# Projections that give way every six matmuls instead of every three, and a shift of 224 bytes in the tiles of the last stage

## The chip, the core and the metric

The program runs on one core of a Trainium2 chip. The metric is the device time of one execution in microseconds (us). Three executions of the kernel before took 650.53, 650.55 and 651.75 us; the median, 650.55 us, is the time before.

## What is computed

One decoder block over 1024 tokens and a width of 1024. An RMS norm is followed by one input projection whose columns feed two groups of heads: eight heads of stick-breaking attention (width 64) and four heads of a gated delta rule (width 128, in chunks). Each group's output is normalised per head and multiplied by a gate; one output projection over both groups, a residual and a last RMS norm end the block.

```python
h = rmsnorm(x, norm1_w)
sb_q, sb_k, sb_v, sb_z, g_q, g_k, g_v, g_z, g_b, g_a = split(h @ w_in)
# attention, strictly causal, per head
z = q @ k.T / 8
attn = where(causal, exp(log_sigmoid(z) - tail), 0)   # tail: suffix sums of softplus(z)
o_sb = rmsnorm(attn @ v, sb_norm_w) * silu(sb_z)
# gated delta rule: conv4 + silu on q, k, v, l2 norms, then chunk after chunk
v_new = u - w @ state
o = (q * exp(g)) @ state + a @ v_new
state = state * exp(g_last) + (k * exp(g_last - g)).T @ v_new
o_gdn = rmsnorm(o, gdn_norm_w) * silu(g_z)
out = rmsnorm(x + concat(o_sb, o_gdn) @ w_out, final_norm_w)
```

## The kernel before

All fp32 products that matter are made of three fp32r matmuls: each operand is split into a high and a low part, and `mm3` adds high times high, high times low and low times high. A projection of 128 columns over 1024 tokens is two halves of 512 tokens, each half eight steps over the contraction (k = 0 to 7), each step one `mm3`: 24 matmuls of 128x512 into one PSUM bank `pp`. In their names `xh` and `xl` are the two parts of the activations, `weh` and `wel` those of the weights.

The order of the work is not written by hand. The kernel is made of generators (streams): the projections (`fill`), the delta rule's loads, preparation, solve and scan, the attention windows (`window`), and the output stage. A planner (`Model` and `interleave`) keeps its own clock and its own costs for every engine. Whenever the planner's PE queue is empty it takes, of the streams that are ready, the one of the lowest number, runs it up to its next `yield`, and records the instructions that it issued; this fixes the order of the instructions on each engine. A stream that yields an operation is ready again only when that operation's result has, by the planner's clock, been there for a slack of 450 ns. The projections have number 100, behind attention (about 10) and the delta rule (0 to 0.7), so that they fill PE where nothing else is ready; the products of the output stage have 101 and 102 and take that part later.

The names that the text uses on PE, the engine of the matmuls:

- `pp<-xh,weh`, `pp<-xl,weh`, `pp<-xh,wel`: projections. The list `ORDER` takes the attention's gates, `z0` to `z3`, last of all.
- `pz<-kh,q` and `pz<-kl,q`: scores of an attention window, `kh` and `kl` against a block of queries. ScalarE and VectorE read them (`sgf`, `cc`), GpSimd multiplies, and PE turns the result: `pz<-step,stf`. `ah` and `al` are its two parts; `po<-ah,v2a` and `po<-al,v2a` multiply them with the values; `pz<-step,otf` turns the output back.
- `pc<-state,kqf`, `pc<-xct,xinv`, `pz<-v,kn`, `pz<-state,kqf`, `pz<-vr,at`: one chunk of the delta scan; between the first three a VectorE operation stands each time.
- `pp<-woh,mh`, `pp<-wol,mh`, `pp<-woh,ml`: the output stage. `mh` and `ml` are parts of the activations (the operand that is loaded into the array), `woh` and `wol` those of the output weights (the operand that streams). The delta half (k = 4 to 7 of the 1024 rows of `w_out`) is multiplied first for all eight blocks of tokens, then the attention half (k = 0 to 3).

The weights of the delta half lie in pool `f0`, those of the attention half in pool `f1`, on the other side of the memory, together with `yj`, a scratch tile for squares, and tiles for the residual. In the built program `mh` and `ml` and the delta half's weights all start at a byte address that leaves 128 when divided by 256; the attention half's eight weight tiles leave 96 (`woh0` is at 133728). Of the projections, `xh`, `xl`, `weh` and `wel` all leave 96.

The line of every instruction that the planner records is 358, so the profile's groups are told apart by the names of their tiles.

Of the kernel before, what the change touches and what calls it, by code (L numbers as in the profile page):

```python
# [10 lines left out]
F32 = mybir.dt.float32  # L11
# [6 lines left out]
P = 128  # L18
# [3 lines left out]
NK = D // P  # L22
# [451 lines left out]
def block(tc, xT_d, x_d, n1_d, wE_d, wQ_d, wC_d, conv_d, alog_d, dtb_d, mixw_d, wo_d, fnw_d, out_d):  # L474
# [4 lines left out]
    with ExitStack() as top:  # L479
# [36 lines left out]
        def rsqrt(y, a, n):  # L516
            return G.tensor_tensor(y, a, half[:, 0:n], ALU.pow)
# [68 lines left out]
        def mm3(out, lh, ll, rh, rl, start, stop):  # L586
            TE.matmul(out, lh, rh, start=start, stop=False)
            TE.matmul(out, lh, rl, start=False, stop=False)
            TE.matmul(out, ll, rh, start=False, stop=stop)
# [176 lines left out]
        def values():  # L766
            for b in range(NB):
                yield lambda: ps.room("pp", 2)
                bs = slice(b * P, (b + 1) * P)
                pt = pp()  # L770
                for k in range(NK):
                    mm3(pt[:, 0:256], xh[:, k, bs], xl[:, k, bs], chl[k][:, 0, 264:520], chl[k][:, 1, 264:520], k == 0, k == NK - 1)
                    if k % 2 and k < NK - 1:
                        yield
                v_evac(pt, b, 0, 4, 1.0)
                yield
            flags["v1"] = True
# [107 lines left out]
        def projections():  # L885
            todo = []
            for step in ORDER:
                if step[0] == "G":
                    h = int(step[1])
                    todo += [(f"G{h}{kind}", lambda: True) for kind in (1, 0, 2)]  # L890
                else:
                    todo.append((step, lambda: True))

            def take():
                for n, (name, ok) in enumerate(todo):
                    if ok():
                        del todo[n]
                        if name[0] == "v":
                            return name, None
                        e = {"k": 0, "z": 16}.get(name[0])  # L900
                        e = 4 + 4 * int(name[2]) + int(name[1]) if name[0] == "G" else e + int(name[1])
                        if e == early.e:
                            return name, early
                        cols = Columns(e)
                        cols.load()
                        return name, cols
                return None

            def split(nxt, n):
                while nxt and nxt[1] and len(nxt[1].hl) < n:  # L910
                    nxt[1].split()

            nxt = take()
            split(nxt, 2)
            while nxt:
                name, cols = nxt
                if name[0] == "v":
                    nxt = take()
                    split(nxt, 2)
                    yield from values()  # L920
                    continue
                fill.prio = 100
                for half in range(2):
                    hs = slice(half * 512, (half + 1) * 512)
                    wide = name[:2] == "G0" and half
                    yield lambda: ps.room("pz", 4) if wide else ps.room("pp", 2)
                    pt = pz() if wide else pp()
                    for k in range(NK):
                        n = 8 * half + k
                        if n == 2:  # L930
                            nxt = take()
                        if n == 8:
                            split(nxt, 1)
                        if n == 12:
                            split(nxt, 2)
                        h, l = cols.hl[k // 4]
                        mm3(pt, h[:, k % 4, :], l[:, k % 4, :], xh[:, k, hs], xl[:, k, hs], k == 0, k == NK - 1)
                        if k < NK - 1:
                            yield
                    if half == 0:  # L940
                        if name[0] == "G":
                            ev = g_evac(int(name[1]), int(name[2]))
                        else:
                            ev = {"k": k_evac, "z": z_evac}[name[0]](int(name[1]))
                    flags[name if half else name + ".0"] = ev(pt, half)
                    yield
                if nxt is None:
                    nxt = take()
                    if nxt is None and todo:
                        yield lambda: any(ok() for _, ok in todo)  # L950
                        nxt = take()
                    split(nxt, 2)
            flags["proj"] = True
# [413 lines left out]
        pools = {}  # L1367
# [55 lines left out]
        def block_tile(b, name):  # L1423
            return pools[0].tile([P, D], F32, tag="xr", bufs=3, name=name) if b < 3 else pools[1].tile([P, D], F32, tag="yr", bufs=5, name=name)
# [88 lines left out]
        def products_attention():  # L1513
            yield lambda: f"d{NB - 1}" in flags
            for b in range(NB):
                last = b == NB - 1
                parts = (slice(0, 512), slice(512, 832), slice(832, D)) if last else (slice(0, 512), slice(512, D))
                sy = None
                for got in product(b, 0, parts):
                    if not isinstance(got, tuple):  # L1520
                        yield got
                        continue
                    n, hs, yp, y = got
                    if sy is None:
                        sy = pools[0].tile([P, 3], F32, tag="sy", bufs=2, name="sy")
                        yf = block_tile(0, "yf") if last else y
                    V.tensor_tensor(y[:, hs], yp, y[:, hs], ALU.add)
                    junk = pools[1].tile([P, 512], F32, tag="yj", name="yj")
                    if n == 2:
                        V.scalar_tensor_tensor(junk[:, 0:hs.stop - hs.start], y[:, hs], 1.0 / D, y[:, hs], ALU.mult, ALU.mult, accum_out=sy[:, n:n + 1])  # L1530
                    else:
                        A.activation(junk[:, 0:hs.stop - hs.start], y[:, hs], AF.Square, scale=D ** -0.5, accum_out=sy[:, n:n + 1])
                    if last and n < 2:
                        G.tensor_tensor(yf[:, hs], y[:, hs], wts["fnw"][:, hs], ALU.mult)
                    if n == 1 and last:
                        G.tensor_tensor(sy[:, 0:1], sy[:, 0:1], sy[:, 1:2], ALU.add)
                    elif n:
                        V.scalar_tensor_tensor(sy[:, 0:1], sy[:, 0:1], EPS, sy[:, n:n + 1], ALU.add, ALU.add)
                    if n < len(parts) - 1:
                        yield  # L1540
                        continue
                    if last:
                        V.tensor_tensor(yf[:, hs], y[:, hs], wts["fnw"][:, hs], ALU.mult)
                    ry = pools[0].tile([P, 1], F32, tag="ry", bufs=2, name="ry")
                    os_ = slice(b * P, (b + 1) * P)
                    if last:
                        rsqrt(ry, sy[:, 0:1], 1)
                        V.tensor_scalar(yf[:, 0:640], yf[:, 0:640], ry[:, 0:1], None, ALU.mult)
                        A.activation(yf[:, 640:D], yf[:, 640:D], AF.Copy, scale=ry[:, 0:1])
                        S.dma_start(out_d[os_, 0:640], yf[:, 0:640])  # L1550
                        nc.scalar.dma_start(out_d[os_, 640:D], yf[:, 640:D])
                    else:
                        rsqrt(ry, sy[:, 0:1], 1)
                        for u in range(2):
                            us = slice(512 * u, 512 * u + 512)
                            yb = (pc, po)[u]()
                            A.activation(yb, y[:, us], AF.Copy, scale=ry[:, 0:1])
                            V.tensor_tensor(y[:, us], yb, wts["fnw"][:, us], ALU.mult)
                        S.dma_start(out_d[os_, :], y)
                    ck.free(*ready[b, 0][:2], y)  # L1560
                    flags[f"a{b}"] = True
                    yield

        fill = Stream(projections(), 100, RESULT)
        pre = Stream(delta_pre(), 0.7, DELTA + 0.7)
        interleave(ck, lambda: ps.room("pz", 4),
# [42 lines left out]
```

## Time and profile before

| | us |
|---|---|
| median of three runs | 650.55 |
| the profiled execution | 650.36 |
| its span, first to last instruction | 648.4 |
| outside the span (650.36 - 648.4) | 2.0 |
| PE busy | 639.2 of 648.4 |
| VectorE (DVE) busy | 423.4 |
| ScalarE (ACT) busy | 393.7 |
| GpSimd (POOL) busy | 341.4 |

The profile is of one execution. PE is the engine of the matmuls, PEld its loading of weights, SP the queue that issues most DMAs. Matmuls are pipelined and their ends are modelled, so the length that the profile gives for one matmul overlaps the next: what a matmul costs is read from the distance between the starts of two that follow each other. A time in the chain of waits, which has no overlap, can be divided by the number of its instructions in the same way.

### The profile page before, as it was taken

The numbers are of one execution on the slowest core, as the hardware profiler recorded it, in microseconds if no ns is written. First come the engines' busy times: TensorE is split into PE (matmuls) and PEld (weight loads), VectorE is DVE, ScalarE is ACT, GpSimd is POOL, SyncE is SP. The second block draws the span as 40 slices with busy tenths as digits, with TensorE's granted clock in tenths as the row PEclk, the third lists the DMA queues.
The fourth block names the chain that finished last, engine by engine and source line by source line (L and its number), as shares of the span: only waits on it lengthen the run. The fifth ranks groups of instructions, "written<-read, shape, count | busy, mean of one in ns | idle before, by whom it ended". The sixth has DMA issues, their size and how long they took to land.

```text
span 648.4 us, 11679 instructions
## 1 busy us (share of the span) xinstructions
PE 639.2 (99%) x3976; PEld 549.7 (85%) x3976; DVE 423.4 (65%) x779; ACT 393.7 (61%) x945; POOL 341.4 (53%) x428
## 2 busy tenths in 40 slices
PE   8999999999999999999999999999999999999996
PEld 7889989988888898888988878888888888888885
DVE  4469974223877869888528887457874326568874
ACT  6664577724967779876559786467854343043553
POOL 0115056837894678835479686287731223226642
PEclk9999999999999999999999999999999999999998
DMA  8976338865383446453463752725312259963312
GB/s 302 324 271 229 133 116 281 285 221 182 106 280 119 129 127 186 133 154 109 121 215 82 263 165 78 225 90 173 109 58 82 82 196 310 346 194 106 123 77 119
DMA packets 96666, 111.82 MB, mean 172 GB/s; under 512 B 28576, under 2 KB 61536, under 8 KB 96608
## 3 DMA queue, kind: packets, MB, share of 16 engines
q1 hardware_dynamic: 96320, 110.89, 52.4%
q8 instruction: 31, 0.51, 0.3%
q14 instruction: 27, 0.22, 0.1%
q10 hardware_dynamic: 288, 0.20, 0.1%
HBM read 76.03 MB, written 35.03 MB: 171 GB/s over the span
## 4 chain that ended last, share of the span: by engine, by line
PE 91%; DVE 4%; issue 1%; ACT 1%; POOL 1%; DMA 1%; POOLq 0%; SPq 0%; DVEq 0%; ACTq 0%
PE pp L358 55%; PE pz L358 26%; PE po L358 7%; PE pc L358 3%; DVE cc L358 1%; DMA kqf<-g_s 1%; ACT sgf L358 0%; DVE al L358 0%; DVE pp L358 0%; POOL sgf L358 0%; DVE wy L358 0%; DVE xr L358 0%; DVE ac L358 0%; POOL wel L358 0%; POOL ac L358 0%
## 5 line engine op out<-in xcount | busy, mean ns | idle before, releaser
L358 PE MATMUL pp<-xh,weh 128*128 128x512 f32 x360 | 150.3, 417 | 0.0
L358 PE MATMUL pp<-xh,wel 128*128 128x512 f32 x360 | 141.5, 393 | 0.0
L358 PE MATMUL pp<-xl,weh 128*128 128x512 f32 x360 | 141.0, 392 | 0.0
L358 POOL TENSOR_TENSOR wel<-wer,weh 128x512 fp32r<-128x512 f32 x48 | 62.8, 1314 | 86.1 <-ACT weh L358 69.7
L358 POOL TENSOR_TENSOR sgf<-sgf,cc 128x128 f32<-128x128 f32 (+3 forms) x64 | 77.3, 1210 | 50.4 <-DVE cc L358 45.0
L358 PEld LDWEIGHTS pp<-xh,wel 128*128 128x128 f32 x360 | 67.6, 188 | 15.2
L358 PEld LDWEIGHTS pp<-xl,weh 128*128 128x128 f32 x360 | 67.9, 189 | 8.6
L358 PEld LDWEIGHTS pp<-xh,weh 128*128 128x128 f32 x360 | 67.7, 188 | 8.7
L358 ACT ACTIVATE sgf<-pz,rs 128x384 f32<-128x384 f32 (+3 forms) x96 | 54.9, 606 | 7.5 <-PE pz L358 7.4
L358 DVE TENSOR_TENSOR_SCAN cc<-pz,step 128x384 f32<-128x384 f32 (+2 forms) x64 | 53.6, 847 | 8.9 <-ACT pz L358 7.4
L358 DVE TENSOR_TENSOR al<-pz,ah 128x512 fp32r<-128x512 f32 (+1 forms) x80 | 49.4, 628 | 13.3 <-ACT ah L358 12.9
L358 ACT ACTIVATE ah<-pz 128x512 fp32r<-128x512 f32 (+1 forms) x80 | 44.4, 572 | 21.0 <-PE pz L358 20.8
L358 ACT ACTIVATE pz<-pz,ns 128x384 f32<-128x384 f32 (+3 forms) x96 | 54.4, 585 | 0.0
L358 PE MATMUL pp<-woh,mh 128*128 128x512 f32 (+2 forms) x132 | 52.1, 394 | 0.0
L358 PE MATMUL pp<-woh,ml 128*128 128x512 f32 (+2 forms) x132 | 51.1, 387 | 0.0
L358 PE MATMUL pp<-wol,mh 128*128 128x512 f32 (+2 forms) x132 | 51.0, 386 | 0.0
L358 DVE SCALAR_TENSOR_TENSOR pp<-pre,conv,pp 128x512 f32<-128x512 f32 x42 | 31.5, 750 | 20.7 <-ACT pp L358 20.3
L358 POOL TENSOR_TENSOR ml<-mf,mh 128x512 fp32r<-128x512 f32 x16 | 22.1, 1380 | 41.2 <-ACT mh L358 35.6
L358 POOL TENSOR_TENSOR ac<-ac,pre 128x512 f32<-128x512 f32 x24 | 31.0, 1292 | 23.3 <-ACT pre L358 13.5
L358 PE MATMUL po<-ah,v2a 128*128 128x256 f32 (+1 forms) x160 | 41.9, 287 | 0.0
L358 DVE TENSOR_TENSOR_SCAN cc<-pz,cc,step 128x512 f32<-128x512 f32 (+1 forms) x32 | 38.8, 1212 | 2.8 <-ACT pz L358 2.4
L358 PE MATMUL po<-al,v2a 128*128 128x256 f32 (+1 forms) x160 | 38.8, 280 | 0.0
(292 smaller groups left out, 1591.8 us busy)
## 6 DMA issues: line engine op xcount, KB each, us to landing
wer<-wE SPq DMA_DIRECT2D x48, 256.0 KB, 3.8
xr<-x SPq DMA_DIRECT2D x16, 512.0 KB, 8.8
g_s<-ac SPq DMA_DIRECT2D x24, 256.0 KB, 2.5
v_s<-v2e SPq DMA_DIRECT2D x16, 256.0 KB, 2.7
kqf<-g_s SPq DMA_DIRECT2D x16, 256.0 KB, 5.3
v2a<-v_s SPq DMA_DIRECT2D x8, 512.0 KB, 5.0
q<-qk_s SPq DMA_DIRECT2D x8, 512.0 KB, 3.8
kh<-qk_s SPq DMA_DIRECT2D x8, 512.0 KB, 5.2
```

Of the source, the lines that this page charges most:

```text
L358: ins = f(*args, **kw).ins
```

## The change

```diff
@@ projections()
                         h, l = cols.hl[k // 4]
                         mm3(pt, h[:, k % 4, :], l[:, k % 4, :], xh[:, k, hs], xl[:, k, hs], k == 0, k == NK - 1)
-                        if k < NK - 1:
+                        if (k%2 or name in ('z0','z1','z2','z3')) and k < NK - 1:
                             yield
@@ products_attention()
                     V.tensor_tensor(y[:, hs], yp, y[:, hs], ALU.add)
-                    junk = pools[1].tile([P, 512], F32, tag="yj", name="yj")
+                    junk = pools[1].tile([P, 568], F32, tag="yj", name="yj")
```

The first line makes every projection but `z0` to `z3` yield after each second step, that is after six matmuls. The number of matmuls, DMAs and operations is the same in both programs. The second line makes the scratch tile 56 floats (224 bytes) longer; no instruction reads or writes the added part. `woh0` moves from byte 133728 to 133504, and with it all eight weight tiles of the attention half now leave 128 when divided by 256, as `mh` and `ml` do.

On PE the planner's order changes from the first projections that run beside other streams to the end of the output stage. In the order before, the 512-wide projection matmuls stand in 172 unbroken runs, 101 of them of three matmuls and 53 of six; in the new order they stand in 126, 5 of three and 101 of six. The groups of transposes that are followed by something else are 128 before and 129 now.

PE, delta scan of the first head, between a chunk's product with the state and the product with the inverse (`pc<-state,kqf` to `pc<-xct,xinv`); VectorE makes `xct` in between. Before:

```order
L358 MATMUL pc<-state,kqf_1094 128x128
L358 MATMUL pz<-kh,q_2044 128x512
L358 MATMUL pz<-kl,q_2044 128x512
L358 MATMUL pz<-kh,q_2044 128x384
L358 MATMUL pz<-kl,q_2044 128x384
L358 MATMUL pp<-xh,weh 128x512
L358 MATMUL pp<-xl,weh 128x512
L358 MATMUL pp<-xh,wel 128x512
L358 MATMUL pp<-xh,weh 128x512
L358 MATMUL pp<-xl,weh 128x512
L358 MATMUL pp<-xh,wel 128x512
L358 MATMUL pc<-xct,xinv 128x128
```

The same place now:

```order
L358 MATMUL pc<-state,kqf_1108 128x128
L358 MATMUL pz<-kqf_2084 128x256 x4
L358 MATMUL pp<-xh,weh 128x512
L358 MATMUL pp<-xl,weh 128x512
L358 MATMUL pp<-xh,wel 128x512
L358 MATMUL pp<-xh,weh 128x512
L358 MATMUL pp<-xl,weh 128x512
L358 MATMUL pp<-xh,wel 128x512
L358 MATMUL pc<-xct,xinv 128x128
```

Both orders have six projection matmuls there; before, the planner gave them in two grants of three, now in one of six, and what it puts beside them is another stream's work.

PE, a little later in the same scan, where attention, scan and projections alternate. Before:

```order
L358 MATMUL pz<-step,stf_2501 128x128 x3
L358 MATMUL pp<-xh,weh 128x512
L358 MATMUL pp<-xl,weh 128x512
L358 MATMUL pp<-xh,wel 128x512
L358 MATMUL pz<-kh,q_2044 128x512
L358 MATMUL pz<-kl,q_2044 128x512
L358 MATMUL pc<-xct,xinv 128x128
L358 MATMUL pz<-step,otf_2760 128x128 x2
L358 MATMUL pp<-xh,weh 128x512
L358 MATMUL pp<-xl,weh 128x512
L358 MATMUL pp<-xh,wel 128x512
L358 MATMUL po<-ah,v2a 128x256
```

And now:

```order
L358 MATMUL pz<-v_2638,kn 128x128
L358 MATMUL pz<-vr,at 128x128
L358 MATMUL pz<-step,otf_2751 128x128 x2
L358 MATMUL pp<-xh,weh 128x512
L358 MATMUL pp<-xl,weh 128x512
L358 MATMUL pp<-xh,wel 128x512
L358 MATMUL pp<-xh,weh 128x512
L358 MATMUL pp<-xl,weh 128x512
L358 MATMUL pp<-xh,wel 128x512
L358 MATMUL pc<-state,kqf_1108 128x128
```

The short runs of three between two other streams are gone; the other streams' pieces follow each other more often, and six projection matmuls follow.

## The prediction

> **What bounds the kernel now.** I read the page's busy times first, then the windows by stage, then PE's waits.
>
> ```profile
> PE 639.2 (99%) x3976; PEld 549.7 (85%) x3976; DVE 423.4 (65%) x779; ACT 393.7 (61%) x945; POOL 341.4 (53%) x428
> PE 91%; DVE 4%; issue 1%; ACT 1%; POOL 1%; DMA 1%; POOLq 0%; SPq 0%; DVEq 0%; ACTq 0%
> ```
>
> ```profile
> 120.00:160.00 40.00, 40.00 (x237) 35.46 (x236) 12.15 (x30) 16.13 (x46) 24.95 (x49) 1.00 0.72 228
> 160.00:200.00 40.00, 39.59 (x245) 32.84 (x244) 33.42 (x58) 31.89 (x80) 31.92 (x34) 1.00 0.55 168
> 360.00:400.00 40.00, 39.40 (x324) 33.51 (x323) 33.21 (x60) 30.21 (x89) 29.31 (x31) 1.00 0.58 177
> 480.00:520.00 40.00, 40.00 (x247) 34.79 (x246) 15.87 (x35) 15.52 (x45) 8.63 (x8) 1.00 0.20 67
> ```
>
> The columns are the stretch, its length, then busy time of PE, PEld, DVE, ACT and POOL, the granted clock, the DMA share and GB/s. PE is busy in all of nearly every stretch at the full clock, and no other engine comes near it. Only 160 to 200 and 360 to 400 us show holes, 0.41 and 0.60 us. The waits on PE agree:
>
> ```profile
> PE po L358 <- DVE step L358: 1.7, 1, 1.7
> PE pz L358 <- DVE dt L358: 0.5, 1, 0.5
> PE pz L358 <- DVE al L358: 0.4, 1, 0.4
> PE pz L358 <- DVE cc L358: 0.2, 1, 0.2
> ```
>
> After the start, 1.1 us of waits are long enough to be listed. The view of one tile counts shorter ones too; before the scores of attention (tile `kh`) PE or its weight loads stood until:
>
> ```profile
>   DVE cc L358: 1.7, 5
>   DVE al L358: 1.1, 2
>   PE pz L358: 0.5, 1
>   DVE oe L358: 0.2, 1
>   DVE state L358: 0.2, 1
> ```
>
> These five make 3.7 us, the largest store of waiting that I found. So the time is the sum of PE's own instructions plus a few us, and the change can act in three ways: on what a matmul costs (the addresses), on how often PE changes from one kind of work to another (the grants), and on those waits (the order).
>
> **The addresses.** The chain of waits has long unbroken pieces of 512-wide matmuls, whose length over their number is the price of one:
>
> ```profile
> 521.51 19.76 PE pp L358 x87
> 566.06 5.57 PE pp L358 x24
> 577.78 11.00 PE pp L358 x48
> 619.18 5.67 PE pp L358 x24
> 625.15 14.08 PE pp L358 x60
> ```
>
> The first are projections (19.76 / 87 = 227 ns), the second and third the delta half of the output stage (5.57 / 24 = 232, 11.00 / 48 = 229 ns), the last two its attention half (5.67 / 24 = 236, 14.08 / 60 = 235 ns). In the timeline the attention half never settles at the projections' distance, though nothing interrupts it:
>
> ```profile
> 625.52 0.40 PE L358 MATMUL pp<-woh,ml 128*128 128x512 f32 x1
> 625.75 0.40 PE L358 MATMUL pp<-woh,mh 128*128 128x512 f32 x1
> ...
> 627.85 0.40 PE L358 MATMUL pp<-woh,mh 128*128 128x512 f32 x1
> ```
>
> Ten matmuls from 625.52 to 627.85 are 233 ns each. The two halves do the same work with the same shapes. DMA doesn't explain it: the delta half runs under the larger share.
>
> ```profile
> 578.00:588.00 10.00, 10.00 (x46) 1.00 0.76 231
> 626.00:638.00 12.00, 12.00 (x53) 1.00 0.32 131
> ```
>
> What differs is where the streamed operand lies: projections and delta half have both operands at the same remainder of 256 bytes, the attention half has 96 against 128. After the change it has 128 against 128. The product groups count how many matmuls this touches:
>
> ```profile
> L358 PE MATMUL pp<-woh,mh 128*128 128x512 f32 x124 | 49.7, 401 | 0.0
> ```
>
> 124 times three is 372; the delta half has 8 blocks x 2 halves x 12 = 192, so the attention half has 180. At 236 - 232 = 4 ns (the groups of 24) the gain is 0.7 us, at 235 - 229 = 5.5 ns (the long pieces) 1.0 us. I take 5 ns, **0.9 us**. The bounds are 0 (the address is not the cause) and 235 - 227 = 8 ns, 1.4 us. A loss would need the new place to be worse than the old; it is the delta half's own place, whose rows are faster. All of it lies on the path: the chain runs on PE up to 639.23 us, after the last of the 180, and the tail behind it keeps its order on every engine.
>
> ```profile
> 629.88 9.35 PE pp L358 x40
> 639.23 0.02 issue
> 639.25 0.04 DVE xr L358
> ```
>
> [...]
>
> **The grants.** 46 unbroken runs of projections fewer (172 to 126), the same instructions. What does one change of work cost? Two kinds of row answer.
>
> ```profile
> 372.54 0.47 PE L358 MATMUL pz<-step,kwf 128*128 128x128 f32 x4
> 372.84 0.46 PE L358 MATMUL pp<-xh,weh 128*128 128x512 f32 x1
> 373.14 0.39 PE L358 MATMUL pp<-xl,weh 128*128 128x512 f32 x1
> 373.37 0.40 PE L358 MATMUL pp<-xh,wel 128*128 128x512 f32 x1
> ...
> 279.09 0.39 PE L358 MATMUL po<-ah,v2a 128*128 128x256 f32 x1
> 279.32 0.28 PE L358 MATMUL po<-al,v2a 128*128 128x256 f32 x1
> 279.43 0.28 PE L358 MATMUL po<-ah,v2a 128*128 128x256 f32 x1
> ```
>
> The first projection after transposes takes 373.14 - 372.84 = 0.30 us instead of 0.23, so entering costs about 0.07 us. But a value product after small matmuls pays as well (0.23 us, then 0.11): whoever follows pays. The transposes come in 128 groups before and 129 now, so this price moves to another stream and is not saved. The second kind is a change without such a price:
>
> ```profile
> 370.68 0.40 PE L358 MATMUL pp<-xh,wel 128*128 128x512 f32 x1
> 370.92 0.40 PE L358 MATMUL pz<-kh,q 128*128 128x512 f32 x1
> 371.16 0.39 PE L358 MATMUL pz<-kl,q 128*128 128x512 f32 x1
> 371.39 0.28 PE L358 MATMUL po<-ah,v2a 128*128 128x256 f32 x1
> ```
>
> The matmuls on both sides of the hand-over take 0.24 us against 0.227, some 13 ns more (two decimals make that uncertain by 10). 46 x 13 ns = **0.6 us** saved. The bounds: 0 if another stream pays this too, and 46 x 0.07 = 3.2 us if the entry price were saved every time, which the count of groups speaks against. I stay near the low end.
>
> **The waits.** A stream that is passed over until a grant ends waits for up to six matmuls, 6 x 0.227 = 1.36 us, instead of 0.68. Behind it stands the rest of that stream: in the scan `xct` on DVE, then `v`, then the next state; in attention the turned weights and the value products. On the other side, each result then has longer to arrive before PE reaches its reader. In the orders, between the scan's product with the inverse and the product with `kn` stand no projection matmuls in 7 places before and 4 now, three in 5 places before and none now, six in 14 before and 23 now. Three give DVE 0.68 us, six 1.36. So I expect less standing on PE, not more: of the 3.7 us I take off **0.5 us**. The bounds are all of it, 3.7 us less, and as much again, 3.7 us more, since the planner's costs are not the chip's and every place has moved. This is the widest unknown.
>
> Does the delay of the streams lengthen the whole? Only if attention or the scan ends after the projections that cover it. In the old order the scan's last product stands just ahead of the row at 521.51, whose 87 projection matmuls and 27 more come behind it, 114 in all. In the new order 126 come behind it, so the scan ends earlier against its cover than before: cost 0. If it were gone, the delta half's products would start late by the scan's delay.
>
> DMAs, evacuations and weight splits are the same in number; SP passes them in another order, at shares of 0.2 to 0.7 in the rows above, and PE shows no wait for weights. Cost 0 while PE is fed; the price of a late weight tile would be a listed wait as above, about 0.5 us.
>
> **The sum.** The profiled execution took 650.36 us for its span of 648.4 (2.0 us outside), 0.19 below the median. 650.36 - 0.9 - 0.6 - 0.5 = 648.36; with the 0.19 added the median should be 648.5 us, 0.3% less. With each term moved by about half, the likeliest case has 647.6 to 649.4.
>
> **The rivals.**
>
> 1. The address is not the cause. For it: only two halves are compared, which also differ in time and in what ACT and POOL do beside them. Against it: the attention half is slow from its first matmul to its last. Then 650.55 - 1.1 = 649.4 us.
> 2. The grants and waits give nothing, because every price moves to another stream, and only the address counts: 650.55 - 0.9 = 649.6 us. The constant number of groups speaks for it.
> 3. The waits mostly vanish, since results have twice the time to arrive: 3 us instead of 0.5, 650.55 - 0.9 - 0.6 - 3 = 646.0 us. Against it: most listed waits are for `cc`, in front of scores, where no projection need stand between.
> 4. Slower: PE stands before scores. With longer grants a window's score pairs follow each other directly (in the first place shown above they already do), and the next pair needs a PSUM bank that DVE's scan `cc` has not yet read out. The rows have 3.7 us of this. It decides once it grows by over 1.5 us, the gain of the other two terms; with 4 us more, about as much again, the time is 650.55 - 1.5 + 4 = 653.1 us. For it: `cc` ends five of those waits. Against it: the planner opens such a pair only when a bank is free by its clock, as before.
>
> **How the numbers follow.** Chances: forecast 0.50, rival 1 0.15, rival 2 0.15, rival 3 0.08, rival 4 0.12. The predicted time is the forecast's, 648.5 us. The range, 646.6 to 651.2 us, holds the forecast and rivals 1 and 2 and leaves out most of 3 and 4. A difference of 0.2%, 1.3 us, is about what a measurement of this kernel can tell; faster therefore means below 649.25, slower above 651.85. Nearly all of the forecast, rival 3 and a third of rival 1 lie below: 0.62. Rival 2, the rest of rival 1 and the forecast's edge are the same: 0.27. Rival 4: 0.11.
>
> **What would show it.** Address: in the attention half's long pieces the price of one falls from 235 to 229 ns; if it stays at 235, rival 1. Grants: the projections' pieces of three vanish from the chain, and PE has about 0.6 us less outside waits; if scores and value products now carry the entry price and PE's sum without waits is unchanged, rival 2. Waits: the list before tile `kh` is at or below 3.7 us; if it is at 6 or more with `cc` first, rival 4. The prediction would be wrong altogether if a listed wait of several us appeared on PE between 160 and 520 us, or if the long piece of projections at 521.51 us, with the output stage behind it, began microseconds later.

## The result, and the profile after

| | before | after |
|---|---|---|
| median of six runs each | 650.54 us | 648.30 us |
| lowest and highest | 650.20 to 651.75 | 647.89 to 648.89 |
| ratio, 95% interval | | 0.9965 (0.9955 to 0.9976) |
| the profiled execution | 650.36 us | 648.05 us |
| its span | 648.4 us | 646.3 us |

The kernel is 0.35% faster. To see where, PE's time is cut at three starts that the timeline shows: the first product of the output stage (548.37 us before, 546.79 after), the first of its attention half, and the last matmul (642.02 and 639.93).

| us | up to the output stage | delta half | attention half |
|---|---|---|---|
| before | 548.37 | 46.51 | 47.14 |
| after | 546.79 | 46.85 | 46.29 |
| difference | -1.58 | +0.34 | -0.85 |

Together -2.09 us, which is the difference of the spans. The tail behind the last matmul is 6.4 us in both. The +0.34 us of the delta half is work that changed its place: of the transposes `pz<-step,mwf`, which turn the blocks, 32 stand in this half now and 28 before, and in the attention half 20 instead of 24. In before a group of four at 571.46 us takes 0.29 us up to the start of the matmul behind it, and that matmul 0.31 us to the next start instead of 0.23.

The attention half first. The chain of waits of after has the pieces that answer to those at 566.06, 577.78, 619.18 and 625.15 us before:

```profile
516.58 19.74 PE pp L358 x87
564.52 5.57 PE pp L358 x24
576.24 8.28 PE pp L358 x36
617.47 5.59 PE pp L358 x24
623.35 13.79 PE pp L358 x60
```

Projections stay at 19.74 / 87 = 227 ns, the delta half at 5.57 / 24 = 232 ns. The attention half falls from 5.67 to 5.59 us for 24 and from 14.08 to 13.79 us for 60, from 235 to 230 ns each: it now has the price of the delta half. Summed by the distances to the next start, its 180 matmuls of 512 columns go from 42.42 to 41.61 us. That is 0.81 of the 0.85 us; the group of transposes that left the half and a wait of 0.27 us at 605.6 us, which is new, cancel but for 0.04.

PE's waits of after, listed and before the scores:

```profile
PE po L358 <- DVE step L358: 1.7, 1, 1.7
PE pp L358 <- DMA mgf<-gate_s: 0.5, 1, 0.5
PE pz L358 <- DVE al L358: 0.2, 1, 0.2
```

```profile
  DVE al L358: 0.7, 3
  DVE cc L358: 0.5, 2
  ACT nkv L358: 0.4, 1
  issue: 0.2, 1
  DVE state L358: 0.2, 1
```

Before the scores PE or its weight loads stood for 3.7 us and now stand for 2.0. The listed waits behind the start went from 1.1 to 0.7 us, and the larger of the two is new: it stands where the output stage begins.

```profile
546.79 0.47 PE L358 MATMUL pp<-woh,mh 128*128 128x512 f32 x1 [0.46 <-DMA mgf<-gate_s]
```

These views leave out waits under 150 ns. To count those too I took, for each matmul, its distance to the next start, and the distance that is usual for the same three kinds of matmul in a row: the one before, this one and the next, told apart by tiles and shape (the lower fifth over all traces of this case). What lies over it by more than 25 ns is counted as waiting, the rest is the price of the work. From the first score to 521 us, **the waits are 5.8 us before and 3.3 after**. Five more traces of the order of after, in the experiments below, give 3.1 to 3.3, one more of the order of before 5.9, so the count repeats within 0.2 us; some expectations quote counts that are higher by as much. The price of the work from the first matmul to the output stage is 540.1 us before and 540.2 after. So all of the gain ahead of the output stage is waiting, and none is the price of changing work: 2.5 us less from the scores on, 0.2 more ahead of them, and 0.6 more where the output stage begins.

The groups by shape show why. The first row of each pair is the projection that is usually the first of a run, the second the value product:

```profile
L358 PE MATMUL pp<-xh,weh 128*128 128x512 f32 x360 | 150.3, 417 | 0.0
...
L358 PE MATMUL po<-ah,v2a 128*128 128x256 f32 x128 | 36.3, 304 | 0.0
```

```profile
L358 PE MATMUL pp<-xh,weh 128*128 128x512 f32 x360 | 147.9, 411 | 0.0
...
L358 PE MATMUL po<-ah,v2a 128*128 128x256 f32 x128 | 38.3, 320 | 0.0
```

The projections give up 2.4 us and the value products take 2.0. Up to the output stage, a projection follows transposes or unsplit fp32 matmuls 120 times before and 85 times now, a value product 36 times before and 58 now, a score 32 and 41 times: 188 such entries before and 184 now. Whoever came next paid for the change, and the number of entries hardly moved.

### The profile page after: what moved, and what is told of

It reads as the page before. It is cut to its first block, busy times and chain, and to the rows that moved or that the text cites. A ratio compares the mean times of both kernels' runs of the same rounds, so it can differ in the third digit from the quotient of the medians.

```text
span 646.3 us, 11666 instructions
## 1 busy us (share of the span) xinstructions
PE 637.6 (99%) x3976; PEld 549.7 (85%) x3976; DVE 425.0 (66%) x779; ACT 394.1 (61%) x945; POOL 339.3 (53%) x428
## 4 chain that ended last, share of the span: by engine, by line
PE 94%; DVE 2%; ACT 1%; issue 1%; POOL 1%; DMA 1%; POOLq 0%; SPq 0%; DVEq 0%; ACTq 0%
PE pp L358 55%; PE pz L358 27%; PE po L358 8%; PE pc L358 3%; DVE mgf L358 1%; POOL rsb L358 1%; DMA mgf<-gate_s 0%; DVE ssb L358 0%; DVE xr L358 0%; DVE mf L358 0%; ACT xinv L358 0%; ACT sgf L358 0%; DMA xr<-x 0%; DVE wol L358 0%; ACT nkv L358 0%
## 5 line engine op out<-in xcount | busy, mean ns | idle before, releaser
L358 PE MATMUL pp<-xh,weh 128*128 128x512 f32 x360 | 147.9, 411 | 0.0
L358 PE MATMUL po<-ah,v2a 128*128 128x256 f32 (+1 forms) x160 | 43.9, 300 | 0.0
```

The lines of the kernel that those rows point to most:

```text
L358: ins = f(*args, **kw).ins
```

## The experiments

The column of waits is the count from the first score to 521 us. Ratios are against the kernel before on the same chip. The stages and the waits are read from one trace of each kernel; the six traces with the order of after reach the output stage between 546.37 and 547.18 us, so differences of a few tenths in that column say little.

| kernel | median us | ratio (95%) | up to output stage | delta half | attention half | waits |
|---|---|---|---|---|---|---|
| before | 650.5 | 1 | 548.37 | 46.51 | 47.14 | 5.8 |
| after | 648.3 | 0.9965 (0.9955-0.9976) | 546.79 | 46.85 | 46.29 | 3.3 |
| shift only | 649.5 | 0.9983 (0.9975-0.9992) | 548.21 | 46.50 | 46.24 | 5.9 |
| grants only | 648.5 | 0.9970 (0.9959-0.9981) | 546.60 | 46.83 | 46.89 | 3.2 |
| all six | 650.4 | 0.9999 (0.9990-1.0007) | 545.62 | 47.19 | 49.09 | 3.4 |
| slack 800, threes | 663.1 | 1.0197 (1.0181-1.0214) | 558.40 | 50.58 | 45.95 | 5.3 |
| slack 550, threes | 648.1 | 0.9963 (0.9949-0.9977) | 547.09 | 46.35 | 46.36 | 3.7 |
| twelves | 650.0 | 0.9997 (0.9987-1.0006) | 545.61 | 47.55 | 48.02 | 2.6 |
| slack 350, sixes | 648.0 | 0.9960 (0.9945-0.9975) | 547.48 | 46.44 | 46.25 | 4.2 |
| threes for z2, z3 only | 647.2 | 0.9947 (0.9932-0.9961) | 546.04 | 46.52 | 46.26 | 3.2 |

### The shift alone

The order of before, on every engine, with the longer scratch tile.

```diff
-                    junk = pools[1].tile([P, 512], F32, tag="yj", name="yj")
+                    junk = pools[1].tile([P, 568], F32, tag="yj", name="yj")
```

> The order of before with the longer scratch tile alone. If the address sets the price of a matmul in the attention half, that half's 180 matmuls go from 42.4 us to about 41.6 us, its long pieces settle at 227 ns, and the time falls by 0.8 us to about 649.7 us; the waits stay as they were. If the address is not the cause and the new order brought the cheaper matmuls, the half stays at 42.4 us and the time at 650.5 us.

649.51 us, 0.9983. The delta half and everything before it are as in the kernel before, waits included; the attention half is 0.90 us shorter. Its chain:

```profile
612.72 5.57 PE pp L358 x24
624.43 13.73 PE pp L358 x60
```

The same order, the same work, 13.73 / 60 = 229 ns instead of 235, and 41.53 us for the 180 matmuls. The address is the cause.

### The grants alone

```diff
-                        if k < NK - 1:
+                        if (k%2 or name in ('z0','z1','z2','z3')) and k < NK - 1:
```

> The order of after with the scratch tile of 512. If the two parts add up, the time is 2.2 - 0.8 = 1.4 us below before, about 649.1 us; the attention half costs 42.4 us as before and PE's waits are those of after. If the gain came from the address alone, the time is that of before.

648.51 us, 0.9970, 2.0 us less than before and somewhat better than expected. In the trace it is the waits that fall, 5.8 to 3.2 us, and the attention half keeps the price of before, 42.40 us for its 180 matmuls (it is 0.25 us shorter only because the group of transposes has left it):

```profile
611.52 5.66 PE pp L358 x24
617.48 5.67 PE pp L358 x24
623.44 14.09 PE pp L358 x60
```

In the medians the two parts, 1.0 and 2.0 us, make more than the 2.2 us of both; the intervals of each are 0.5 us or wider on either side, so the medians can't tell whether anything is lost. The traces show one small thing: in after, with the cheaper matmuls, PE has to wait some 0.27 us at 605.6 us, where a block is turned in the attention half, and at that place some 0.05 us in this kernel.

### Which addresses are equal enough

Four kernels with the order of after; the scratch tile sets where the weights lie, and in the last one the tile ahead of the activations is made longer instead.

```diff
# weights at 0, at 224, and 512 apart: three kernels
-                    junk = pools[1].tile([P, 568], F32, tag="yj", name="yj")
+                    junk = pools[1].tile([P, 536], F32, tag="yj", name="yj")
...
+                    junk = pools[1].tile([P, 544], F32, tag="yj", name="yj")
...
+                    junk = pools[1].tile([P, 632], F32, tag="yj", name="yj")
# activations moved, junk back at 512
-            fv = pools[0].tile([P, 512], F32, tag="mf", name="mf")
+            fm = pools[0].tile([P, 568], F32, tag="mf", name="mf")
+            fv = fm[:, 0:512]
```

> After, with the scratch tile at 536 floats: the attention half's weights leave 0 when divided by 256, the activations 128. If equal remainders by 256 are what counts, its 180 matmuls go back to about 42.4 us with long pieces at 232 to 235 ns. If multiples of 128 are enough, they stay at 41.6 us.

> After, with the scratch tile at 544 floats: the attention half's weights leave 224, the activations 128, a difference of 96. If equal remainders by 256 are what counts, the half costs about 42.4 us; if only some differences are bad, it may stay at 41.6 us.

> After, with the scratch tile at 632 floats: the weights leave 128 when divided by 256 as the activations do, but 128 against 384 when divided by 512. If 256 bytes are the period, the half costs 41.6 us as in after; if the period is 512 or more, it costs about 42.4 us.

> After with the scratch tile at 512, so that the attention half's weights leave 96 as in before, and with the activations of the output stage moved by 224 bytes to the same remainder 96 (the tile ahead of them made longer). Of the delta half, the weights of rows 4 to 6 keep 128 and differ now, those of row 7 move along. If equal remainders are what counts, the attention half costs 41.6 us, and 144 of the delta half's 192 matmuls get dearer by some 5 ns, 0.7 us in all. If the place of the streamed weights itself counts, the attention half costs 42.4 us and the delta half stays.

Each ran once beside the kernel before; the single times (648.39, 649.03, 648.53 and 648.36 us) are too near each other to rest on, the chains are not. The piece of 60 matmuls in the attention half with the weights at 0, at 224, and equal by 256 but not by 512, in this order, one kernel each:

```profile
623.36 14.02 PE pp L358 x60
```

```profile
623.79 14.08 PE pp L358 x60
```

```profile
623.75 13.77 PE pp L358 x60
```

A difference of 128 bytes (14.02) and of 96 (14.08) is about as dear as the 32 of before (14.08); equal by 256 is cheap (13.77), though the two differ by 512. Other differences were not tried. Of the last kernel, first a piece of the delta half and then two of the attention half:

```profile
564.40 5.66 PE pp L358 x24
...
611.95 5.54 PE pp L358 x24
...
623.70 13.76 PE pp L358 x60
```

Here the streamed weights of the attention half are where they were before the change, and are cheap because the activations came to them. The delta half, whose weights did not move for three of four rows, pays now: 5.66 us for 24 instead of 5.57, and 45.28 us instead of 44.50 summed over its 192 matmuls' distances. In these kernels it is the equality of the two operands' remainders by 256 that counts, not the place of either.

### The exception for the last projections

After, with sixes for `z0` to `z3` too.

```diff
-                        if (k%2 or name in ('z0','z1','z2','z3')) and k < NK - 1:
+                        if k%2 and k < NK - 1:
```

> After, but z0 to z3 also give way every six matmuls, so the exception is undone. If longer grants are good because results get more time, the last projections gain a little too: 648.0 us or the same 648.3 us. If at the end of the projections the late stages (scan end, first turned blocks of the output stage) need PE soon, a wait of about 0.5 us or more appears between 480 and 550 us and the time is 649 us or above.

650.42 us: the whole gain is gone. The output stage is reached earlier, at 545.62 us instead of 546.79, and then takes 96.28 us instead of 93.14. The listed waits:

```profile
PE pz L358 <- issue: 1.1, 1, 1.1
PE pp L358 <- DVE xr L358: 1.0, 2, 0.8
PE pp L358 <- POOL ml L358: 0.3, 1, 0.3
```

I had expected a wait where the projections end. The waits stand later, mostly in the attention half, for blocks that are not yet prepared (the turn, `pz`, and `ml`) and for DVE, which is late with `xr`, the sum with an earlier product: DVE's first scaling of an attention block (`mgf<-mgf,rsb`) starts at 582.44 us in after (first row) and at 587.76 us here (second, another kernel).

```profile
582.44 0.68 DVE L358 TENSOR_TENSOR mgf<-mgf,rsb 128x512 f32<-128x512 f32 x1
```

```profile
587.76 0.68 DVE L358 TENSOR_TENSOR mgf<-mgf,rsb 128x512 f32<-128x512 f32 x1
```

A last kernel keeps the threes for `z2` and `z3` alone.

```diff
-                        if (k%2 or name in ('z0','z1','z2','z3')) and k < NK - 1:
+                        if (k%2 or name in ('z2','z3')) and k < NK - 1:
```

> After, but only z2 and z3 give way every three matmuls. The run without any exception reached the output stage 1.2 us earlier than after and lost 3.1 us in it. If the loss comes from the last two projections, beside which the output stage's first blocks are turned, this keeps the gain: about 647 to 648 us. If it is already lost with z0 and z1, the output stage takes about 96 us as in the run without exception and the time is about 650.4 us.

647.15 us, 0.9947, the fastest kernel here, 1.1 us under after: all its four times (646.80 to 647.38) lie below all six of after, though on another chip, and the intervals of the two ratios overlap. The output stage takes 92.78 us, the waits for DVE and POOL are gone, and so is the wait for the gate that after has at the entry:

```profile
PE po L358 <- DVE step L358: 1.7, 1, 1.7
PE pz L358 <- DVE al L358: 0.2, 1, 0.2
```

So the exception is worth about 3 us, and two of its four projections carry it. This kernel's own first scaling starts at 584.38 us. Counted from the start of the output stage it begins 35.7 us on in after, 38.3 here and in before, 40.2 with the slack of 550 ns below, and 42.1 with sixes throughout: the kernels at up to 40 us show no such waits, those at 42 us (the twelves below too) do. Why the planner comes to it later when the last two projections take sixes was not settled.

### Is it time for results to arrive?

Grants of three and a longer slack in the planner give results more time too, without longer grants. The shifted tile is in both kernels.

```diff
-SLACK = 450
+SLACK = 800
```

> The order is planned with grants of three as before, but a stream is ready only 800 ns after its result is there by the planner's clock, not 450; the shifted tile is in it. If the gain of the grants is time for results to arrive, this gives the same without longer grants: PE's short waits fall from 6.6 to about 4.8 us and the time is about 648.3 us. If the gain is fewer changes of work on PE, the waits fall but the time stays near 649.7 us, that of the shift alone.

663.12 us, which is the number of neither case: PE stands for 9 us in one place.

```profile
PE pz L358 <- DVE mgf L358: 9.1, 1, 9.1
PE pp L358 <- issue: 1.8, 1, 1.8
...
539.65 0.39 PE L358 MATMUL pz<-vr,at 128*128 128x128 f32 x2
```

The last row is the scan's last product: it stands at 539.65 us with 30 projection matmuls behind it, where before has 114 and after 126. The output stage's first weights and blocks are loaded after the scan, and 30 matmuls, 7 us, don't cover that. This is the price that the prediction named for cover that is gone. It is more than the wait: in the 8 us to 564 us, behind it, the granted clock of PE (third from the end of the row) is 0.50, and PE has 19 matmuls in 6.07 us of busy time, against 32 in the 6.00 us of the next row. The delta half takes 50.58 us, 4.1 more than with the shift alone; how much of that is the clock was not separated.

```profile
556.00:564.00 8.00, 6.07 (x19) 4.31 (x20) 5.82 (x16) 1.67 (x2) 1.28 (x1) 0.50 1.08 365
564.00:570.00 6.00, 6.00 (x32) 4.90 (x31) 3.14 (x5) 1.33 (x3) 2.59 (x2) 0.97 1.03 410
```

All this hides what was asked, so the slack was set to 550 ns, with which the order leaves 138 behind the scan.

```diff
-SLACK = 450
+SLACK = 550
```

> Grants of three as before, the shifted tile, and a slack of 550 ns in the planner; by the order the scan ends with 138 projection matmuls behind it, so the cover that the run with 800 ns lost is there. If the gain of the longer grants is time for results to arrive, PE's waits from the first score to 521 us fall clearly below the 6.0 us of the shift alone, towards the 3.3 us of after, and the time is about 648.5 us. If longer grants do something else, the waits stay near 5 to 6 us and the time near 649.5 us.

648.12 us, 0.9963, the time of after, with runs of three still the rule. The waits are 3.7 us, and those before the scores fall as in after:

```profile
  DVE al L358: 0.7, 3
  DVE cc L358: 0.5, 1
  ACT wy L358: 0.3, 1
  ACT sgf L358: 0.2, 1
```

Against the shift alone 2.2 us of waiting are gone, while the price of the work up to the output stage rises by 0.5 us, to 540.5. So the gain does not need longer grants. The other way round, sixes with less slack:

```diff
# of after
-SLACK = 450
+SLACK = 350
```

> After with a slack of 350 ns instead of 450. If the long grants already give results their time, less slack costs little: waits of 3.3 to 4 us and 648.3 us. If the planner's slack still decides, the waits go back up towards 6 us and the time to 650 us or above.

647.95 us, 0.9960: the waits rise from 3.3 to 4.2 us, about a third of the way back, and the time stays, since the wait at the entry of the output stage is absent in this order. The long grant gives most of the time that the slack gave.

### Grants of twelve

```diff
# of after
-                        if (k%2 or name in ('z0','z1','z2','z3')) and k < NK - 1:
+                        if (k%4 == 3 or name in ('z0','z1','z2','z3')) and k < NK - 1:
```

> After, but with grants of twelve matmuls (z0 to z3 still three): 92 unbroken runs instead of 126. If fewer changes of work were worth 13 ns each, as the prediction has it, this gains another 0.4 us; if the price only moves to another stream, nothing. If time for results counts, the waits fall below 3.3 us. The scan then has 87 projection matmuls behind it instead of 126, still some 20 us: if the output stage needs more than that, a wait of some us stands at its start and the time is over 649 us.

650.00 us. The waits are the lowest of all, 2.6 us, and this time the price of the work falls as well, 539.0 us up to the output stage instead of 540.2; it is reached at 545.61 us. Then the output stage takes 2.4 us more than in after, with waits for what ACT, DVE and POOL prepare:

```profile
PE pp L358 <- ACT mh L358: 1.0, 1, 1.0
PE pp L358 <- DVE xr L358: 0.8, 1, 0.8
PE pp L358 <- POOL ml L358: 0.7, 1, 0.7
```

Two of them, 1.0 and 0.7 us, stand at its start, where the expectation put the wait for a cover that is too short; whether the cover or the place of the turns in the order makes them was not separated:

```profile
545.61 0.50 PE L358 MATMUL pp<-woh,mh 128*128 128x512 f32 x1 [0.97 <-ACT mh L358]
545.96 0.39 PE L358 MATMUL pp<-wol,mh 128*128 128x512 f32 x1
547.02 0.50 PE L358 MATMUL pp<-woh,ml 128*128 128x512 f32 x1 [0.67 <-POOL ml L358]
```

In after 0.46 us stands there. The rest is lost later: the first scaling begins 42.5 us into the output stage, as late as with sixes throughout. Of the 1.2 us in the price of the work, about 0.3 is a group of four transposes that now comes after the start of the output stage. The other 0.9 us go with a count: 158 entries behind transposes or unsplit fp32 matmuls here, 184 in after, 188 in before. The change moved entries from one stream to another, the twelves removed 26. No run varied this count alone, so that it sets the price is likely and not shown.

## Why the prediction was right, and where it was not

The predicted time, 648.5 us, is 0.2 us from the median, and the range holds it. That it came so near is luck: one of the three terms failed, another was five times too small, and new waits, which the sum had at 0, took back most of the difference.

**The addresses: right.** The forecast was 0.9 us. The half's 180 matmuls take 0.81 us less in after and, at an unchanged order, 0.89 less with the shift alone. The bounds came from pieces of 24 and 48 to 60 matmuls, and 5 ns was the price. Rival 1, that the halves differ for another reason, is refuted by the shift alone and by the moved activations. Of the pairs tried only those with equal remainders by 256 are cheap: the piece of 60 takes 13.72 to 13.79 us with both at 128 and 13.76 with both at 96, and 14.02 to 14.09 us with weights at 0, 96 or 224 against activations at 128.

**The grants: wrong.** The step that failed is "46 x 13 ns = 0.6 us saved". It took the price of a hand-over from matmuls on both sides of one change and assumed that with fewer runs of projections there are fewer hand-overs to pay. Measured up to the output stage the price of the work is 540.1 us before and 540.2 after. The text had the reason in hand, since it argued that the entry price of 0.07 us moves to whoever follows, and the two groups, 2.4 us less and 2.0 us more, fit that, with 188 entries before and 184 after. Rival 2 was right on this term.

**The waits: the direction right, the size too small.** The forecast took 0.5 us; the waits from the first score to 521 us fell by 2.5 us, and the new one at the entry gave some 0.6 us back (0.46 by the view). The argument from the orders, that six matmuls give a result 1.36 us where three gave 0.68, holds: with the shift in both, slack alone buys 0.9963 with threes where the long grants buy 0.9965. It was counted low because 0.5 was taken of the 3.7 us before the scores, of which 1.7 went, while short waits elsewhere went too. Rival 3, with 3 us, came near to what the waits did ahead of the output stage. Rival 4, PE standing before scores for `cc`, did not happen: those waits went from 1.7 to 0.5 us.

**The cover: right.** The scan was to end earlier against its cover. The long piece of projections behind it begins at 516.58 us instead of 521.51, and the run with a slack of 800 ns shows what it costs when the cover is gone: 9 us of standing, and more behind it.

**What was not seen.** The prices of a late tile at the entry of the output stage were put at about 0.5 us and taken as 0; one such wait came. And in the output stage itself the orders of these kernels differ by up to 3.6 us with the cover in place (92.69 to 96.28 us), which no part of the prediction speaks of. The sum came out because errors cancel: 2.0 us more of waits went than the forecast took off, but the 0.6 us of the grants did not come, and waits of 0.6 us at the entry, 0.27 us in the attention half and 0.2 us ahead of the first score were added.

## What to carry to other kernels

When one engine is busy for 99% of the span, compare the price of equal instructions between stages, by start distances: here a stage stayed at 235 ns where others had 227 to 232, the cause was where its operands lie, and moving its weights by 224 bytes took it to 230 ns and cost nothing. Fewer runs of the filler, 126 instead of 172, saved nothing in the price of the work (540.2 us and 540.1 before), since the next stream paid for the change; what a longer grant or a little more slack bought is time for results, with waits of 3.3 and 3.7 us instead of 5.8. With 30 projection matmuls as cover behind the scan, where after has 126, a stand of 9.1 us cost more than that. After any such edit look at the stage behind it first: here sixes for all projections, and twelves, reached the output stage 1.2 us earlier and lost 2 to 3 us in it.

## What the runs showed of the hardware that was not expected

In the traces of before and after a 512-wide fp32r matmul behind transposes does not go back to the projections' 227 ns at once, and with unequal addresses it does not do so within the piece. The distances between starts, in ns, in the attention half's piece of 60 behind a group of transposes, before and after the change:

```
before: 305 230 235 231 235 232 235 232 235 231 235 232 235 232 235 231 235 232 235 231 235 232
after:  302 235 233 236 224 231 236 228 233 231 226 227 227 226 227 227 226 227 227 226 227 227
```

With equal remainders by 256 the first distance is 75 ns longer, some nine more are uneven, at about 232 ns, and from then on it is 226 and 227. In after a single distance of 259 ns at 628.75 us starts such a course once more: six uneven ones, 228 to 236, then 226 and 227. With unequal remainders the distance swings between 231 and 235 ns to the end of the piece. The narrower pieces of the last block show none of this: its 320-wide matmuls take 146 ns before and 147 after at the median, the 192-wide ones 111 in both.

With the slack of 800 ns the granted clock is 0.50 from 556 to 564 us, behind the stand of 9.1 us, and 0.97 in the 6 us that follow. The mean clock of that kernel's four executions is 0.989 or 0.990, where those with the shift alone have 0.997 to 0.999. Whether the stand brought the lower clock was not tested by itself.
